# Hybrid decoder trunk, one core: the second merged half turned by VectorE and HBM, the output projection in eight banks and two halves

## The chip, the core and the metric

The program runs on one core of one Trainium2 chip. The core has TensorE (PE in the profile, with PEld for its weight loads), VectorE (DVE), ScalarE (ACT), GpSimd (POOL) and SyncE (SP), which here only issues DMAs. Each engine works through its own list of instructions in order; semaphores make one engine wait for another. PSUM has eight banks of 128 x 512 fp32 values, and TensorE's results land there. The metric is device time in microseconds of one execution, lower is better.

## The reference, cut to what matters

Two layers work on x, 256 tokens by 1024 channels, fp32. A layer is

```python
h = rms_norm(x, attn_norm[l])
p = h @ w_in[l]                                  # split into the branches' inputs and three gates
merged = (sigmoid(g_mla) * (o_mla @ w_branch_mla)
          + sigmoid(g_moba) * (o_moba @ w_branch_moba)
          + sigmoid(g_ret) * (o_ret @ w_branch_ret))
x = x + merged @ w_out[l]                        # the output projection: 256 x 1024 by 1024 x 1024
h = rms_norm(x, mlp_norm[l])
x = x + squared_relu(h @ w_up) @ w_down
```

and a last rms_norm follows. The change touches `merged`, of which the retention branch is the last term, and `merged @ w_out`.

## The kernel before, in words

**Numbers.** fp32 products are made of three passes: each operand is split into a high part (ScalarE, a copy to the type fp32r) and the rest (VectorE, a subtraction), and `three` (L298 to L300) issues high by high, high by low, low by high. A matmul takes a 128 x 128 stationary tile and up to 512 moving columns.

**Weights.** `weight_plan` lays all weights out in HBM in blocks of at most 128 x 1024 fp32 (512 KB), in the order of use. `fetch` brings one block: SP issues the transfer into a `raw` buffer (L210, seven buffers), ScalarE makes `whi` (L277), VectorE makes `wlo` (L279), six buffers each. `load_w` hands a block out and fetches ahead by `AHEAD`; `have(n)` fetches until n blocks are ready or on the way. A raw buffer is free again when its `wlo` is made, a `whi` buffer when TensorE has used the block. `behind[key]` is a list of instructions: when block `key` is fetched, what it issues on the same engine is put behind them (`tc.issue_after`).

**Order.** Instructions are traced in program order; a scheduler then orders each engine's list by a simulated time, those traced earlier first when several are ready. `tc.keep_in_program_order(ins)` puts an instruction behind the one traced before it on its engine. `tc.manual_schedule(engines={PE})` keeps TensorE's order as traced while it is open. `prog` is the list of units of a layer and `at(slot, step)` hangs a step behind a unit.

**The stage in question.** Layer 0 reaches it at about 199 us and layer 1 at about 594 us. Merged is made in two halves of 512 channels. For each half the three branches run (`branch`, six units `bmla0` ... `bret1` of two weight blocks each; t is the half of the tokens, j the weight block, kk one of its two 128-row parts). After the retention branch `merge` adds the branch to the merged half (L715 and L717, on VectorE, once for each t); the result is the tile `th`, tokens on partitions. The projection needs merged with channels on partitions, that is turned.

- The first half is turned by VectorE in 32 x 32 blocks (`turn_row`, L328), written to HBM (`bounce`, L342) and read back in the right places (`mergedturned`, four reads, L348). `merged_split` splits it into `mT[0]` (L319).
- The second half is turned by TensorE: `merged_turn(t)` makes four transposes (L1174) into a PSUM tile `pmt`; ScalarE and VectorE split that into `mT[1]` (L319).
- `wout_first` takes the first four of eight column blocks n (128 columns each, `FIRST`, a weight block `wout n` each): the first half of merged for n = 0 to 3, with `merged_turn(0)` behind n = 1 and `merged_turn(1)` behind n = 2, then the second half for n = 0 to 3, each in its own `acc` bank. `out_part` (L1240) issues, for one n and one half, four matmuls of 512 columns (mT's high and low part side by side, by `whi`) and four of 256 (high by `wlo`); for n = 0 it issues twelve of 256, so that the sum needs no second addition.
- `wout(n)` for n = 4 to 7 takes both halves at once, in banks from `acc` (four banks in all).
- `out_done(n)` adds the bank to x (L1244, VectorE, one instruction for n = 0, two else) and takes the MLP's split input `xs` from it (L314 on ScalarE, L315 on VectorE) and its squares (L382, L385, and L387 and L389 for their sum).
- TensorE's order is as traced from `bret1` to the end of `wout_first`; behind it the scheduler mixes `wout` 4 to 7 with the first MLP blocks (`up`, tile `pup`).

The banks are four of tag `acc` and four of tag `misc`.

Of the kernel before, what the change touches and what calls it, by code (L numbers as in the profile page):

```python
# [7 lines left out]
F32 = mybir.dt.float32  # L8
# [62 lines left out]
def weight_plan():  # L71

    plan = []

    def block(key, name, kt, cols, per):
        for j in range(0, kt, per):
            plan.append(((*key, j // per), name, (j, per), cols))

    def span(c, n):
        return range(c, c + n)  # L80

    for l in range(L):
        if l == 0:

            plan.append(((l, "mq", 0), "w_in", (0, 1), C_MQ))
            plan.append(((l, "b0", 0), "w_in", (0, 1), C_MLA))
            for k in range(1, KD):
                plan.append(((l, "b0mq", k), "w_in", (k, 1), [*C_MLA, *C_MQ]))
        else:
            block((l, "b0"), "w_in", KD, C_MLA, 2)  # L90
            block((l, "mq"), "w_in", KD, C_MQ, 2)
        block((l, "mk"), "w_in", KD, C_MK, 2)
        block((l, "mv"), "w_in", KD, C_MV, 2)
        mv, plan = plan[-4:], plan[:-4]
        for i, (key, name, kt, cols) in enumerate(
            (("qrope", "mla_w_q_up", 2, C_QROPE), ("qnope", "mla_w_q_up", 2, C_QNOPE), ("kvup", "mla_w_kv_up", 1, C_KV))
        ):
            block((l, key), name, kt, cols, kt)
            plan.append(mv[i])
        plan.append(mv[3])  # L100
        for i in range(2):
            block((l, "gmla%d" % i), "w_in", KD, span(C_GMLA + 512 * i, 512), 2)
        for i in range(2):
            block((l, "gmoba%d" % i), "w_in", KD, span(C_GMOBA + 512 * i, 512), 2)
        def branch_block(name, i):
            block((l, "b%s%d" % (name, i)), "w_branch_" + name, 4, span(512 * i, 512), 2)

        block((l, "rqk"), "w_in", KD, C_RQK, 2)
        block((l, "rv"), "w_in", KD, C_RV, 2)
        block((l, "rg"), "w_in", KD, span(C_RG, 512), 2)  # L110
        for i in range(2):
            block((l, "gret%d" % i), "w_in", KD, span(C_GRET + 512 * i, 512), 2)
        for name, i in LATE:
            branch_block(name, i)
        for n in range(KD):
            block((l, "wout", n), "w_out", KD, span(P * n, P), KD)
        for kind, i in mlp_order(l):
            if kind == "up":
                g, j = divmod(i, 4)
                plan.append(((l, "up", g, j), "w_mlp_up", (2 * j, 2), span(512 * g, 512)))  # L120
            else:
                plan.append(((l, "down", i, 0), "w_mlp_down", (i, 1), range(D)))
    at, offset = {}, 0
    for key, name, (j, n), cols in plan:
        at[key] = (offset, n, len(cols))
        offset += P * n * len(cols)
    return plan, at, offset
# [22 lines left out]
def trunk(ctx: ExitStack, tc: tile.TileContext, gx, wts, consts, gfin, gn, xtok, out):  # L150
# [35 lines left out]
    def load_w(*key):  # L186

        ahead = 0 if key[:2] in ((0, "b0"), (0, "mq"), (0, "b0mq")) else AHEAD
        have(min(ahead + 1, len(loaded) + len(order)))
        return loaded.pop(key)  # L190
# [94 lines left out]
    def acc_tile(name="acc"):  # L285
        return ps.tile([P, 512], F32, name=name, tag="acc", bufs=4)

    def misc_tile(name="misc"):
        return ps.tile([P, 512], F32, name=name, tag="misc", bufs=4)
# [28 lines left out]
    def split_plain(src, hi, lo):  # L318
        return nc.scalar.activation(hi, src, AF.Copy), nc.vector.tensor_sub(lo, src, hi.bitcast(F32))  # L319
# [371 lines left out]
    def branch(l, key, parts, oT, th, merged, between=None, then=None):  # L691


        def unit(half, j, accs):
            if j == 0:
                accs.extend(acc_tile() for _ in range(NT))
            if between and half and j == 0:
                between(0)
            wh, wl = load_w(l, f"{key}{half}", j)
            by_k = [(t, kk) for kk in range(2) for t in range(NT)]  # L700
            for t, kk in sorted(by_k) if j else by_k:
                if between and half and j and (t, kk) == (0, 0):
                    between(1)
                if between and half and j and (t, kk) == (1, 0):
                    between(2)
                k, sl = 2 * j + kk, slice(P * t, P * t + P)
                three(accs[t], oT[0][:, k, sl], oT[1][:, k, sl], wh[:, kk, :], wl[:, kk, :], k == 0, k == 3)
                if then and j and kk:
                    then(half, t, [tc.keep_in_program_order(step) for step in merge(half, t, accs[t])])
            for t in range(NT) if j and not then else ():  # L710
                list(merge(half, t, accs[t]))

        def merge(half, t, acc):
            z = th[half, t]
            yield nc.vector.scalar_tensor_tensor(z, z, 1.0, acc, op0=ALU.add, op1=ALU.mult)  # L715
            if (half, t) in merged:
                yield nc.vector.tensor_add(merged[half, t], merged[half, t], z)  # L717
            else:
                merged[half, t] = z

        for half in parts:
            accs = []
            for j in range(2):
                prog.append(((f"{key}{half}", j), lambda half=half, j=j, accs=accs: unit(half, j, accs)))
# [60 lines left out]
    def layer(l, xn, before):  # L785
# [379 lines left out]
        th_ret = gates(l, "gret", xn)  # L1165
        order_out = ExitStack()

        def merged_turn(t):
            if t == 0:

                mT.append(sb.tile([P, 4, 2, S], F32R, name="mT", tag="KK", bufs=1))
            pt = misc_tile("pmt")
            for i in range(4):
                nc.tensor.transpose(pt[:, P * i : P * i + P], merged[1, t][:, P * i : P * i + P], ident)  # L1174
            split_plain(
                pt.rearrange("p (k s) -> p k s", k=4), *(mT[1][:, :, i, P * t : P * t + P] for i in range(2))
            )

        def between(i):

            if i == 0:
                order_out.enter_context(tc.manual_schedule(engines={mybir.EngineType.PE}))

        early = []

        def merged_tile(half, t, steps):


            if half:
                behind.setdefault((l, "wout", 5, 0), []).extend(steps[-1:])  # L1190
                return
            if t == 0:
                early.append(blocks_tile("merged"))
            turned = tc.keep_in_program_order(turn_row(early[0], t, merged[0, t]))
            if t == 1:
                behind[l, "bret1", 0] = [turned]
                early.append(turned_by_hbm(early[0], "merged", "t4", T4, (l, "wout", 5, 0)))

        def merged_split():
            mT.append(sb.tile([P, 4, 2, S], F32R, name="mT", tag="Q", bufs=1))  # L1200
# [25 lines left out]

        xm = []

        def out_part(w, acc, half, wide, n=4):


            ks = [(k, mT[k // 4][:, k % 4]) for k in range(4 * half, 4 * half + n)]
            if wide:
                jobs = [(acc, w[0][:, k, :], m.rearrange("p two s -> p (two s)")) for k, m in ks]
                jobs += [(acc[:, :S], w[1][:, k, :], m[:, 0, :]) for k, m in ks]
            else:
                jobs = [(acc[:, :S], w[i][:, k, :], m[:, 0, :]) for k, m in ks for i in range(2)]
                jobs += [(acc[:, :S], w[0][:, k, :], m[:, 1, :]) for k, m in ks]
            for i, (o, a, b) in enumerate(jobs):
                nc.tensor.matmul(o, a, b, start=half == 0 and i == 0, stop=4 * half + n == KD and i == len(jobs) - 1)  # L1240

        def out_done(n, acc):
            for i in range(2 if n else 1):
# [2 lines left out]
                )  # L1246
            xm[0].take(n)

        def wout(n):
            w, acc = load_w(l, "wout", n, 0), acc_tile()  # L1250
            out_part(w, acc, 0, True, KD)
            out_done(n, acc)

        def wout_first():
            xm.append(Normed(G_MLP + KD * l, KD))
            some = [(load_w(l, "wout", n, 0), acc_tile()) for n in range(FIRST)]
            for half in range(2):
                for n, (w, acc) in enumerate(some):
                    out_part(w, acc, half, n > 0)
                    if half == 0 and n in (1, 2):  # L1260
                        merged_turn(n - 1)
            for n in range(FIRST):
                out_done(n, some[n][1])
            order_out.close()

        prog.append((("wout", 0), wout_first))
        for n in range(FIRST, KD):
            prog.append((("wout", n), lambda n=n: wout(n)))
        run()
        xm = xm[0]  # L1270

# [321 lines left out]
W2K = 17  # L1593
WARM = 8
SMALL = 16
FIRST = 4
AHEAD = 1
GAP = 8

# [90 lines left out]
```

## Time and profile before

| what | us |
|---|---|
| time, median of 3 runs | 802.19 (801.83 to 802.56) |
| the profiled execution's own time | 801.34 |
| its span, first to last instruction | 799.2 |
| TensorE busy | 792.5 |
| VectorE busy | 655.9 |
| ScalarE busy | 493.4 |
| TensorE's transposes of the second half, 16 of them, first and last start | 206.7 and 604.2 |

Times in views are microseconds from the span's start, and durations of one instruction stand beside them. Matmuls overlap: one of 512 columns takes 0.39 us from start to end, and the next starts 0.23 us after it. So the cost of a matmul is read from the distance of starts, or from the chain of work that ended last, which counts each only for the time that it adds. The SP queue's rows show when a transfer is issued; the table of DMA issues has the median time from issue to landing.

### The profile page before, as it was taken

The numbers are of one execution on the slowest core, as the hardware profiler recorded it, in microseconds if no ns is written. First come the engines' busy times: TensorE is split into PE (matmuls) and PEld (weight loads), VectorE is DVE, ScalarE is ACT, GpSimd is POOL, SyncE is SP. The second block draws the span as 40 slices with busy tenths as digits, with TensorE's granted clock in tenths as the row PEclk, the third lists the DMA queues.
The fourth block names the chain that finished last, engine by engine and source line by source line (L and its number), as shares of the span: only waits on it lengthen the run. The fifth ranks groups of instructions, "written<-read, shape, count | busy, mean of one in ns | idle before, by whom it ended". The sixth has DMA issues, their size and how long they took to land.

```text
span 799.2 us, 11136 instructions
## 1 busy us (share of the span) xinstructions
PE 792.5 (99%) x3818; PEld 659.2 (82%) x3818; DVE 655.9 (82%) x1131; ACT 493.4 (62%) x750; POOL 29.0 (4%) x32
## 2 busy tenths in 40 slices
PE   9999999999999999999999999999999999999997
PEld 7888887888888888888888888888888888888885
DVE  6789678878888888887796976788698879899785
ACT  7786665544557666665477865654545666666563
POOL 0100000000030000000020000000000300000000
PEclk9999999999999999999999999999999999999999
DMA  9969968965677876776745989598666687688751
GB/s 333 375 229 298 305 224 233 312 217 174 222 218 236 283 224 229 265 265 223 251 163 197 289 281 301 181 280 252 221 231 183 195 284 262 223 287 297 265 185 53
DMA packets 70280, 194.74 MB, mean 244 GB/s; under 512 B 8016, under 2 KB 27856, under 8 KB 70224
## 3 DMA queue, kind: packets, MB, share of 16 engines
q1 hardware_dynamic: 69648, 193.17, 73.6%
q10 hardware_dynamic: 576, 0.87, 0.3%
q8 instruction: 30, 0.49, 0.3%
q14 instruction: 26, 0.21, 0.1%
HBM read 171.46 MB, written 22.02 MB: 242 GB/s over the span
## 4 chain that ended last, share of the span: by engine, by line
PE 99%; DVE 0%; issue 0%; ACT 0%
PE acc L298 19%; PE acc L300 19%; PE acc L299 19%; PE pup L298 8%; PE pup L300 8%; PE pup L299 8%; PE acc L1240 6%; PE acc L859 1%; PE ps_s L1005 1%; PE po L645 1%; PE ps_s L551 1%; PE warm L765 0%; PE po L647 0%; PE ps_r L551 0%; PE b L866 0%; PE b L865 0%
## 5 line engine op out<-in xcount | busy, mean ns | idle before, releaser
L277 ACT ACTIVATE whi<-raw 128x1024 fp32r<-128x1024 f32 (+3 forms) x263 | 264.8, 1019 | 164.6 <-PE acc L300 101.4
L279 DVE TENSOR_TENSOR wlo<-raw,whi 128x1024 fp32r<-128x1024 f32 (+3 forms) x263 | 305.3, 1176 | 70.2 <-ACT whi L277 66.7
L298 PE MATMUL acc<-whi,xs 128*128 128x512 f32 (+1 forms) x384 | 150.0, 392 | 0.0
L299 PE MATMUL acc<-wlo,xs 128*128 128x512 f32 (+1 forms) x384 | 149.4, 389 | 0.0
L300 PE MATMUL acc<-whi,xs 128*128 128x512 f32 (+1 forms) x384 | 149.0, 389 | 0.0
L299 PE MATMUL pup<-wlo,xs 128*128 128x512 f32 x256 | 99.8, 390 | 0.0
L300 PE MATMUL pup<-whi,xs 128*128 128x512 f32 x256 | 99.6, 389 | 0.0
L298 PE MATMUL pup<-whi,xs 128*128 128x512 f32 x256 | 99.4, 389 | 0.0
L298 PEld LDWEIGHTS acc<-whi,xs 128*128 128x128 f32 x384 | 72.1, 188 | 15.7 <-ACT whi L277 0.7
L300 PEld LDWEIGHTS acc<-whi,xs 128*128 128x128 f32 x384 | 72.1, 188 | 14.3
L299 PEld LDWEIGHTS acc<-wlo,xs 128*128 128x128 f32 x384 | 72.1, 188 | 14.0
L300 PE MATMUL acc<-whi,sq 128*128 128x512 f32 x184 | 71.9, 391 | 0.0
L298 PE MATMUL acc<-whi,sq 128*128 128x512 f32 x184 | 71.8, 390 | 0.0
L299 PE MATMUL acc<-wlo,sq 128*128 128x512 f32 x184 | 71.6, 389 | 0.0
L300 PEld LDWEIGHTS pup<-whi,xs 128*128 128x128 f32 x256 | 48.1, 188 | 9.9
L299 PEld LDWEIGHTS pup<-wlo,xs 128*128 128x128 f32 x256 | 48.1, 188 | 9.9
L298 PEld LDWEIGHTS pup<-whi,xs 128*128 128x128 f32 x256 | 47.9, 188 | 9.7
L300 PEld LDWEIGHTS acc<-whi,sq 128*128 128x128 f32 x184 | 34.5, 188 | 7.8 <-DVE sq L319 0.6
L299 PEld LDWEIGHTS acc<-wlo,sq 128*128 128x128 f32 x184 | 34.5, 188 | 7.2
L573 ACT ACTIVATE prob<-prob,smx 128x128 f32<-128x128 f32 x64 | 28.4, 444 | 19.6 <-DVE smx L570 19.5
L298 PEld LDWEIGHTS acc<-whi,sq 128*128 128x128 f32 x184 | 34.6, 188 | 6.9
L1240 PE MATMUL acc<-mT,whi 128*128 128x512 f32 (+1 forms) x144 | 35.2, 371 | 0.0
(278 smaller groups left out, 1204.0 us busy)
## 6 DMA issues: line engine op xcount, KB each, us to landing
raw<-wts SPq DMA_DIRECT2D x264, 512.0 KB, 5.0
bounce<-hblocks SPq DMA_DIRECT2D x16, 512.0 KB, 3.8
hturned<-bounce SPq DMA_DIRECT2D x64, 128.0 KB, 3.1
pbounce<-blocks SPq DMA_DIRECT2D x8, 768.0 KB, 5.8
probT<-pbounce SPq DMA_DIRECT2D x32, 192.0 KB, 5.5
raw<-wts SPq DMA_DIRECT2D x5, 464.0 KB, 6.1
raw<-wts SPq DMA_DIRECT2D x4, 416.0 KB, 4.7
dec<-consts SPq DMA_DIRECT2D x2, 768.0 KB, 7.7
```

The costliest lines, as they stand in the source:

```text
L277: fetched.append(nc.scalar.activation(hi[:, cs], raw[:, cs], AF.Copy))
L279: nc.vector.tensor_sub(lo[:, cs], raw[:, cs], hi[:, cs].bitcast(F32))
L298: nc.tensor.matmul(o, ah, bh, start=start, stop=False, **more)
L299: nc.tensor.matmul(o, ah, bl, start=False, stop=False, **more)
L300: nc.tensor.matmul(o, al, bh, start=False, stop=stop, **more)
L551: mm = nc.tensor.matmul(bank[:, o], a[rows, sa], b[rows, sb_], start=True, stop=True)
L573: nc.scalar.activation(p[:, a:b], p[:, a:b], AF.Exp, bias=m[:, 2 + i : 3 + i], scale=d**-0.5, accum_out=m[:, 4 + i : 5 + i])
L645: nc.tensor.matmul(dst, vh, pT[h + j][0], start=True, stop=False)
L859: nc.tensor.matmul(mq[t][:, cs], a[:, P * t : P * t + P], wq[part][:, cs], start=first, stop=stop)
L1005: nc.tensor.matmul(bank[:, o], mla["Q"][:, h, qs], mla["K"][:, h, ks], start=True, stop=True)
L1240: nc.tensor.matmul(o, a, b, start=half == 0 and i == 0, stop=4 * half + n == KD and i == len(jobs) - 1)
```

## The change

It has four parts.

1. **Last branch by rows.** `bret1` now keeps both weight blocks (`ws`): with the first block it works on token half t = 0 alone, with the second it finishes t = 0 and then does all of t = 1. The sum of t = 0 is complete twelve matmuls before the end of the branch, where it was six.
2. **Second half turned by VectorE and HBM.** For each t, `merged_tile` turns the merged half in 32 x 32 blocks into `late` (one instruction, behind the additions), and SP writes it to HBM (256 KB). `late_fetch` reads it back, four reads of 64 KB for each t, in pieces of 128 values (512 bytes); all reads stand behind the second write in SP's list. `late_split` splits it into `mT[1]`, ScalarE's part behind the `whi` of weight block (1, 1). The eight transposes on TensorE in each layer, and the PSUM tile `pmt`, are gone.
3. **Output projection in eight banks.** Weight blocks are cut anew: four for the first half of merged and four for the second, each with 256 columns. TensorE does the first half of merged for all eight n, then the second half for all eight, in four `misc` and four `acc` banks, and `out_done(n)` follows each n of the second half.
4. **Order.** The manual order of TensorE's list reaches from `bret1` to the end of the projection; `up` blocks no longer come between. `behind` of block (1, 1), sixth of the eight like `wout 5` before, holds the first half's write and both turns, where it held the first half's write and the additions.

```diff
-        for n in range(KD):
-            block((l, "wout", n), "w_out", KD, span(P * n, P), KD)
+        for half in range(2):
+            for m in range(KD // 2):
+                plan.append(((l, "wout", half, m), "w_out", (4 * half, 4), span(2 * P * m, 2 * P)))
...
-            if between and half and j == 0:
-                between(0)
-            wh, wl = load_w(l, f"{key}{half}", j)
-            by_k = [(t, kk) for kk in range(2) for t in range(NT)]
-            for t, kk in sorted(by_k) if j else by_k:
...
-                k, sl = 2 * j + kk, slice(P * t, P * t + P)
+            if between and j == 0:
+                between()
+            ws[half, j] = load_w(l, f"{key}{half}", j)
+            if not between:
+                jobs = [(t, j, kk) for t in range(NT) for kk in range(2)]
+                jobs = jobs if j else sorted(jobs, key=lambda job: job[2])
+            else:
+                jobs = [(t, i, kk) for t, i in ((1, 0), (1, 1)) for kk in range(2)] if j else []
+                jobs = [(0, j, kk) for kk in range(2)] + jobs
+            for t, i, kk in jobs:
+                k, sl = 2 * i + kk, slice(P * t, P * t + P)
+                wh, wl = ws[half, i]
...
             if half:
-                behind.setdefault((l, "wout", 5, 0), []).extend(steps[-1:])
+                if t == 0:
+                    late.append(blocks_tile("merged"))
+                cs = slice(2 * S * t, 2 * S * t + 2 * S)
+                turn = nc.vector.transpose(late[0][:, cs].rearrange("p (b j e) -> p j b e", b=4, j=4), merged[1, t])
+                tc.keep_in_program_order(turn)
+                late.append(dr.tile([P, 2 * S], F32, name="mbounce", bufs=NT))
+                wrote.append(nc.sync.dma_start(late[-1], late[0][:, cs]))
+                behind.setdefault((l, "wout", 1, 1), []).append(turn)
                 return
...
+        def late_fetch():
+            turned = sb.tile([P, 4 * S], F32, name="mergedturned", tag="t4", bufs=T4)
+            for t in range(NT):
+                cs = slice(2 * S * t, 2 * S * t + 2 * S)
+                for b in range(4):
+                    src = late[1 + t].rearrange("(a p) (b r) -> b p a r", a=4, b=4)[b]
+                    with tc.issue_after(wrote[1].ins):
+                        nc.sync.dma_start(turned[32 * b : 32 * b + 32, cs].rearrange("p (a r) -> p a r", a=4), src)
+            return turned
+
+        def late_split(turned):
+            mT.append(sb.tile([P, 4, 2, S], F32R, name="mT", tag="KK", bufs=1))
+            have(2)
+            with tc.issue_after(fetched[-1].ins):
+                for t in range(NT):
+                    src = turned[:, 2 * S * t : 2 * S * t + 2 * S].rearrange("p (a j e) -> p j a e", a=4, j=4)
+                    split_plain(
+                        src,
+                        *(mT[1][:, :, i, P * t : P * t + P].rearrange("p j (a e) -> p j a e", a=4) for i in range(2)),
+                    )
+
+        def wout():
             xm.append(Normed(G_MLP + KD * l, KD))
-            some = [(load_w(l, "wout", n, 0), acc_tile()) for n in range(FIRST)]
+            turned = late_fetch()
+            accs = [misc_tile("pwo") if n < 4 else acc_tile() for n in range(KD)]
             for half in range(2):
-                for n, (w, acc) in enumerate(some):
-                    out_part(w, acc, half, n > 0)
-                    if half == 0 and n in (1, 2):
-                        merged_turn(n - 1)
-            for n in range(FIRST):
-                out_done(n, some[n][1])
+                for m in range(KD // 2):
+                    w = load_w(l, "wout", half, m)
+                    for i in range(2):
+                        n = 2 * m + i
+                        out_part(w, accs[n], half, n > 0, slice(P * i, P * i + P))
+                        if half:
+                            out_done(n, accs[n])
+                if half == 0:
+                    late_split(turned)
             order_out.close()
```

More of the change, by code (lines that the diff above doesn't have):

```diff
@@ L691, in branch @@
     def branch(l, key, parts, oT, th, merged, between=None, then=None):
+        ws = {}
         def unit(half, j, accs):
@@ L696, in unit @@
                 accs.extend(acc_tile() for _ in range(NT))
-            if between and half and j == 0:
-                between(0)
-            wh, wl = load_w(l, f"{key}{half}", j)
-            by_k = [(t, kk) for kk in range(2) for t in range(NT)]
-            for t, kk in sorted(by_k) if j else by_k:
[L702 to L705, printed above, removed]
-                k, sl = 2 * j + kk, slice(P * t, P * t + P)
+            if between and j == 0:
[10 more added lines that the diff above has]
+                wh, wl = ws[half, i]
                 three(accs[t], oT[0][:, k, sl], oT[1][:, k, sl], wh[:, kk, :], wl[:, kk, :], k == 0, k == 3)
-                if then and j and kk:
+                if then and k == 3:
                     then(half, t, [tc.keep_in_program_order(step) for step in merge(half, t, accs[t])])
@@ L1166, in layer, with between @@
         order_out = ExitStack()
[L1168 to L1184, printed above, removed]
+        def between():
+            order_out.enter_context(tc.manual_schedule(engines={mybir.EngineType.PE}))
+        early, late, wrote = [], [], []
         def merged_tile(half, t, steps):
             if half:
-                behind.setdefault((l, "wout", 5, 0), []).extend(steps[-1:])
+                if t == 0:
[6 more added lines that the diff above has]
+                behind.setdefault((l, "wout", 1, 1), []).append(turn)
                 return
@@ L1196, in merged_tile @@
                 behind[l, "bret1", 0] = [turned]
-                early.append(turned_by_hbm(early[0], "merged", "t4", T4, (l, "wout", 5, 0)))
+                early.append(turned_by_hbm(early[0], "merged", "t4", T4, (l, "wout", 1, 1)))
         def merged_split():
@@ L1227, in layer, with out_part @@
         xm = []
-        def out_part(w, acc, half, wide, n=4):
-            ks = [(k, mT[k // 4][:, k % 4]) for k in range(4 * half, 4 * half + n)]
+        def out_part(w, acc, half, wide, cs):
+            ks = [(k, mT[half][:, k]) for k in range(4)]
             if wide:
-                jobs = [(acc, w[0][:, k, :], m.rearrange("p two s -> p (two s)")) for k, m in ks]
-                jobs += [(acc[:, :S], w[1][:, k, :], m[:, 0, :]) for k, m in ks]
-            else:
-                jobs = [(acc[:, :S], w[i][:, k, :], m[:, 0, :]) for k, m in ks for i in range(2)]
-                jobs += [(acc[:, :S], w[0][:, k, :], m[:, 1, :]) for k, m in ks]
+                jobs = [(acc, w[0][:, k, cs], m.rearrange("p two s -> p (two s)")) for k, m in ks]
+                jobs += [(acc[:, :S], w[1][:, k, cs], m[:, 0, :]) for k, m in ks]
+            else:
+                jobs = [(acc[:, :S], w[i][:, k, cs], m[:, 0, :]) for k, m in ks for i in range(2)]
+                jobs += [(acc[:, :S], w[0][:, k, cs], m[:, 1, :]) for k, m in ks]
             for i, (o, a, b) in enumerate(jobs):
-                nc.tensor.matmul(o, a, b, start=half == 0 and i == 0, stop=4 * half + n == KD and i == len(jobs) - 1)
+                nc.tensor.matmul(o, a, b, start=half == 0 and i == 0, stop=half == 1 and i == len(jobs) - 1)
         def out_done(n, acc):
@@ L1247, in out_done @@
             xm[0].take(n)
[L1249 to L1254, printed above, removed]
+        def late_fetch():
[7 more added lines that the diff above has]
+            return turned
@@ L1262, in wout_first @@
-            for n in range(FIRST):
-                out_done(n, some[n][1])
+                for m in range(KD // 2):
[7 more added lines that the diff above has]
+                    late_split(turned)
             order_out.close()
-        prog.append((("wout", 0), wout_first))
@@ L1267, in layer @@
-        for n in range(FIRST, KD):
-            prog.append((("wout", n), lambda n=n: wout(n)))
+        prog.append((("wout", 0), wout))
         run()
@@ L1595 @@
 SMALL = 16
-FIRST = 4
 AHEAD = 1
```

## The prediction

> **What bounds the kernel now.** I read the page first, then TensorE's waits, then the chain that ended last inside the stage, then the other engines' timelines there.
>
> ```profile
> span 799.2 us, 11136 instructions
> PE 792.5 (99%) x3818; PEld 659.2 (82%) x3818; DVE 655.9 (82%) x1131; ACT 493.4 (62%) x750; POOL 29.0 (4%) x32
> ...
> PE 99%; DVE 0%; issue 0%; ACT 0%
> ```
>
> ```profile
> PE warm L765 <- PEq L1683: 0.8, 1, 0.8
> ```
>
> The chain is TensorE for 99% of the span, and the list of its waits holds this one row, at the start. Of the 6.7 us that TensorE isn't busy (799.2 - 792.5), 0.8 is that wait and most of the rest the end of the program. So nothing can be won but the time of TensorE instructions that are dropped, and any wait put into TensorE's list is lost in full. The stage itself, layer 0, in the chain (start, us, what):
>
> ```profile
> 204.03 2.84 PE acc L1240 x20
> 206.86 0.44 PE pmt L1174 x4
> 207.30 1.40 PE acc L1240 x8
> 208.70 0.44 PE pmt L1174 x4
> 209.14 9.85 PE acc L1240 x60
> ...
> 219.45 5.57 PE acc L1240 x32
> ...
> 225.96 2.77 PE acc L1240 x16
> ```
>
> The reader is to see that each start is the one before plus its time: from the end of the last branch at 204.03 on, projection and transposes follow each other with no gap (the row left out is the first two MLP matmuls). Layer 1 has the same stage 395.4 us later:
>
> ```profile
> 599.43 2.84 PE acc L1240 x20
> ```
>
> Whatever holds for one layer counts twice.
>
> **What is removed.** Two groups of four transposes at 0.44 us: 0.88 us in each layer, 1.76 us in all. That is the whole gain on offer. The work that split `pmt` lay beside matmuls and is replaced by splits of the same shapes.
>
> **What is moved on TensorE.** The projection keeps its columns, but n = 4 to 7 are cut into halves. A half for one n costs 1.40 us (the row of 8 matmuls), so two cost 2.80; both halves at once take 2.77 to 2.79 (16 in 2.77, 32 in 5.57). At 0.01 to 0.03 for each of four n that is up to 0.1 us a layer; against it, `up` matmuls no longer come between projection groups, worth a few hundredths. I take 0.08 lost. The branch's matmuls only change order, and each still accumulates into its bank three at a time and starts 0.23 us behind the one before (203.64 and 203.86 below). Net: 0.80 us a layer gained, 1.6 in all, if nothing waits.
>
> **What is added, and the one wait that matters.** The second half of merged must now be turned, written, read and split before TensorE has done the first half for all eight n. That first half takes 2.84 for n = 0 and 1, and six times 1.40: 11.24 us. TensorE issued the branch's last matmul at 203.64 and the projection's first at 203.86:
>
> ```profile
> 203.64 0.39 PE L300 MATMUL acc<-whi,oretl 128*128 128x512 f32 x1
> 203.86 0.28 PE L1240 MATMUL acc<-mT,whi 128*128 128x256 f32 x1
> 203.98 0.28 PE L1240 MATMUL acc<-mT,wlo 128*128 128x256 f32 x1
> ```
>
> So `mT[1]` is wanted at 215.10: the high part at once, for both t. n = 0 uses the high part in its first eight matmuls, 0.12 us apart, and the low part from 216.06. Now the chain to it, with VectorE's list of before:
>
> ```profile
> 187.83 0.71 DVE L328 STREAM_TRANSPOSE mergedblocks<-th 128x512 f32<-128x512 f32 x1
> 188.47 0.65 DVE L715 SCALAR_TENSOR_TENSOR th<-th,acc 128x512 f32<-128x512 f32 x1
> ```
>
> ```profile
> 201.68 1.28 DVE L319 TENSOR_TENSOR mT<-mergedturned,mT 128x512 fp32r<-128x512 f32 x2
> 202.88 1.22 DVE L279 TENSOR_TENSOR wlo<-raw,whi 128x1024 fp32r<-128x1024 f32 x1
> 204.02 0.68 DVE L715 SCALAR_TENSOR_TENSOR th<-th,acc 128x512 f32<-128x512 f32 x1
> 204.73 0.69 DVE L717 TENSOR_TENSOR th<-th 128x512 f32<-128x512 f32 x1
> 205.34 0.68 DVE L715 SCALAR_TENSOR_TENSOR th<-th,acc 128x512 f32<-128x512 f32 x1
> 206.06 0.69 DVE L717 TENSOR_TENSOR th<-th 128x512 f32<-128x512 f32 x1
> 206.67 1.22 DVE L279 TENSOR_TENSOR wlo<-raw,whi 128x1024 fp32r<-128x1024 f32 x1
> ```
>
> One t costs VectorE, start to start, 0.71 for the gate, 0.61 for the sum (204.02, 204.73, 205.34) and 0.64 for the turn (187.83 to 188.47): 1.96. The bank of t = 0 is now complete twelve matmuls before the end, at 204.03 - 12 x 0.23 = 201.3. Its chain is pinned behind the splits of `mT[0]`, after which VectorE is free at 202.88, and being traced earlier it goes before the `wlo` that stood there. So t = 0 runs 202.88 to 204.84, t = 1 from there to 206.80, its turn ending 0.07 later (0.71 for 0.64). The two weight splits follow; TensorE needs those blocks at 215.1 and 217.9, so their delay is hidden.
>
> Then SP. No row has these transfers; the nearest:
>
> ```profile
> bounce<-mergedblocks SPq DMA_DIRECT2D x2, 512.0 KB, 2.9
> mergedturned<-bounce SPq DMA_DIRECT2D x8, 128.0 KB, 3.1
> ...
> qkoth<-qr SPq DMA_DIRECT2D x8, 64.0 KB, 2.1
> ...
> y<-y SPq DMA_DIRECT2D x2, 256.0 KB, 2.5
> ```
>
> ```profile
> 193.93 1.75 SPq L348 DMA_DIRECT2D mergedturned<-bounce  x4
> ```
>
> The write of 256 KB lies between 2.5 (same size, alone) and 2.9 (512 KB): I take 2.5, issued at 206.9, landed 209.4. The reads of t = 0 are issued while it flies. Those of t = 1 start at 209.4; four issues take 1.75, so the last starts 1.31 after the first, at 210.7. A read lies between 2.1 (64 KB) and 3.1 (128 KB, in the same scattered pattern); I take 3.1, the nearer pattern: landed 213.8. Then the splits:
>
> ```profile
> L319 ACT ACTIVATE mT<-pmt x4: 599/599/600, 207.3 to 604.6; 128x512 fp32r<-128x512 f32 x4
> L319 DVE TENSOR_TENSOR mT<-pmt,mT x4: 692/692/693, 208.0 to 605.2; 128x512 fp32r<-128x512 f32 x4
> ```
>
> High part ready at 213.8 + 0.6 = 214.4, low part at 215.1. Against 215.10 and 216.06 that leaves 0.7 and 1.0 us. With the short ends the spare is 1.7, with the long end of the write 0.3. **No wait, but by less than one VectorE instruction of 1.2 us.**
>
> **What is late next.** During the second half VectorE must run eight `out_done` (rows of the tile x and of `xs`, ns):
>
> ```profile
> L1244 DVE SCALAR_TENSOR_TENSOR GX<-acc,GX x7: 416/417/425, 212.0 to 221.2; 128x256 f32<-128x256 f32 x7
> L315 DVE SCALAR_TENSOR_TENSOR xs<-GX,xs x4: 476/482/977, 214.6 to 224.4; 128x256 fp32r<-128x256 f32 x4
> ```
>
> 15 additions at 0.42 and eight splits at 0.48 are about 10 us, and four `wlo` at 1.14 (202.88 to 204.02) 4.6: some 14 us in 11.2, a little less where neighbours overlap. It falls behind by about 3 us. This is covered: the first `up` block wants only `xs` 0 and 1, and each further pair is wanted 2.7 us later (twelve matmuls at 0.23). Without this cover the price would be those 3 us a layer. The weights have more cover: SP sends a block when a `raw` buffer is free, and the transfers in the stage left room (columns: span, PE, PEld, DVE, ACT, POOL, clock, DMA share, GB/s):
>
> ```profile
> 204.00:216.00 12.00, 12.00 (x81) 10.93 (x80) 8.51 (x15) 6.18 (x9) 0.00 (x0) 1.00 0.47 150
> 216.00:229.00 13.00, 13.00 (x74) 11.35 (x73) 13.00 (x22) 8.71 (x15) 5.12 (x4) 1.00 0.78 239
> ```
>
> The added 512 KB out and 512 KB in each layer fall where DMA is busy 0.47 of the time. SP itself now stands about 3 us for each wait on a write; behind it are weight loads for blocks that TensorE wants 10 us later.
>
> **A page that speaks against it.** The reads were 3.1 us in the same pattern with runs of 1 KB. The Trainium skill, VectorE: DVE Perf Modes, section The three transpose paths, says that a plain DMA which turns by strides is 19 times slower than the chip's transpose path when the innermost destination stride is large. The trace speaks for the kernel: VectorE has turned the blocks, the DMA moves whole runs, 512 bytes here.
>
> **The rivals.**
> *A. The reads stand behind weight loads (slower).* SP's reads of t = 1 wait for the write until 209.4. In that time two weight splits end (206.8 + 1.14 and + 2.28: 208.0 and 209.1), each freeing a `raw` buffer, and SP sends a load at once when one is free, as here right behind the `wlo` of 206.67:
>
> ```profile
> 207.91 0.33 SPq L210 DMA_DIRECT2D raw<-wts  x1
> ```
>
> If the scheduler put loads between write and reads, each moves the reads by its 512 KB, 1.40 us at the rate of the second, fastest slice, 375 GB/s:
>
> ```profile
> GB/s 333 375 229 298 305 224 233 312 217 174 222 218 236 283 224 229 265 265 223 251 163 197 289 281 301 181 280 252 221 231 183 195 284 262 223 287 297 265 185 53
> ```
>
> One load uses up the spare and 0.7 more; two cost 2.1 a layer; three 3.5. From a wait of 0.80 a layer the change loses, from 1.6 by more than 0.2%: two loads give 801.34 - 1.6 + 4.2 = 803.9, three 806.7. For it: the times meet. Against it: the reads are traced before those loads, and elsewhere SP stands idle between write and read rather than slip a load in, 3.2 us on average:
>
> ```profile
> SPq L348 <- DMA bounce<-hblocks: 51.8, 16, 4.5
> ```
>
> A wait has a second price. The matmuls of the start were paced 0.44 us apart for the same 512 columns that later go every 0.23 (3.54 us for eight):
>
> ```profile
> 0.78 3.54 PE warm L765 x8
> ```
>
> The Trainium skill, TensorE: Matmul & The Clock Gate, section What's actually happening, has the clock halved after an idle window of about 3.4 us; by it, a wait that long would cost another 1.7 us, an estimate. Only three loads or more come near it.
>
> *B. Partly given back.* One weight split (1.14 us) gets between the chains of t = 0 and t = 1, or one load before the reads: high part 0.4 to 0.7 late, gain left 0.1 to 0.4 a layer, 800.6 to 801.1 for this execution.
>
> *C. A second half of TensorE work is dearer than counted*, or `xs` comes late after all: the 3 us of VectorE's backlog would then show before `up`. Up to 3 us a layer, 805.7. Against it: 8 us of cover for the last pair.
>
> *D. The reads are slow of themselves.* The slowest scattered read of the table is this one:
>
> ```profile
> probT<-pbounce SPq DMA_DIRECT2D x32, 192.0 KB, 5.5
> ```
>
> At 5.5 us the high part is there at 216.8, 1.7 late: 801.34 - 1.6 + 3.4 = 803.1. Against it: three times the bytes. By the rule of the Trainium skill, VectorE: DVE Perf Modes, The three transpose paths, nineteen times 0.17 us (64 KB at 375 GB/s) for eight reads would be 26 us, an estimate that ends near 840; the 3.1 us of the same pattern leave it no more than 1 in 100.
>
> **How the numbers follow.** Forecast: 801.34 - 1.6 = 799.7 for an execution like the profiled one; that one lay 0.85 under the median of the three runs (802.19), so for the median 800.6. A measurement of this kernel can tell about 0.2%, 1.6 us, from no change: the forecast stands on that line, and half of its chance falls on each side. Forecast, no wait: 0.55 (own range 800.0 to 801.1 for the median), of it 0.30 faster and 0.25 same. B: 0.22, all but 0.02 same. A: 0.14, slower 0.12. C: 0.01 and D: 0.03, slower (D by a hair). Something gained that I don't see, such as a shorter end of the stage: 0.05, faster. Sums: faster 0.37, same 0.47, slower 0.16. The range reaches down to 799.5 and up to A with two loads, 804.8 for the median (803.9 + 0.85).
>
> **What would show it.** The tile `pmt` gone and TensorE's list of waits still one row: the forecast. A row in that list for L1240 behind ScalarE's or VectorE's `mT`, from `mergedturned`, about 10 us after each last branch: A or B; SP's timeline between `mbounce` and `mergedturned` tells which, by a `raw` row there. VectorE's two turns at about 204.2 and 206.2, with or without a `wlo` between, show whether the start of my chain holds. A landing time over 3.1 us for the reads, or over 2.9 for the write, would break it.

## The result, and the profile after

| | before | after |
|---|---|---|
| median | 802.00 us (801.80 to 802.56, 5 runs) | 810.91 us (809.69 to 813.09, 5 runs) |
| ratio, 95% interval | | 1.0114 [1.0104, 1.0125] |
| profiled execution, its span | 801.34, 799.2 us | 809.69, 807.5 us |

The change makes the kernel 1.1% slower, 6 us beyond the upper end of the range. The page of the changed kernel, its first two lines and the chain that ended last:

```profile
span 807.5 us, 11138 instructions
PE 795.6 (99%) x3802; PEld 659.7 (82%) x3802; DVE 659.3 (82%) x1135; ACT 494.3 (61%) x750; POOL 27.2 (3%) x32
...
PE 91%; DMA 3%; DVE 1%; ACT 1%; issue 1%; SPq 1%; POOL 0%; POOLq 0%; ACTq 0%
```

TensorE was 99% of the chain and is now 91%: the end hangs on transfers and on the other engines for some stretches. TensorE has 16 instructions less, the transposes, and yet 3.1 us more of busy time. Its list of waits (total, times, longest) says where:

```profile
PE acc L299 <- ACT sq L320: 4.8, 2, 2.4
...
PE pwo L1238 <- ACT mT L320: 0.2, 1, 0.2
PE acc L301 <- DVE sq L320: 0.2, 1, 0.2
```

The wait that the prediction was about, for `mT`, is the second row shown, and small. The first row isn't in the projection at all. It is the first `down` of the MLP in each layer, 40 us later, which waits for `sq`, the squared hidden values of the first group. The matmuls there (start, us; in brackets the idle time and what ended it), and the same stretch by windows (columns as in the prediction; the number behind POOL's (x0) is the granted clock):

```profile
254.66 0.39 PE L301 MATMUL pup<-whi,xs 128*128 128x512 f32 x1
257.48 0.66 PE L299 MATMUL acc<-whi,sq 128*128 128x512 f32 x1 [2.43 <-ACT sq L320]
...
258.74 0.79 PE L301 MATMUL acc<-whi,sq 128*128 128x512 f32 x1 [0.17 <-DVE sq L320]
259.33 0.63 PE L299 MATMUL acc<-whi,sq 128*128 128x512 f32 x1
259.75 0.63 PE L300 MATMUL acc<-wlo,sq 128*128 128x512 f32 x1
```

```profile
254.00:257.50 3.50, 1.07 (x6) 0.57 (x4) 1.35 (x3) 1.14 (x2) 0.00 (x0) 1.00 1.05 237
257.50:261.00 3.50, 3.33 (x7) 2.17 (x8) 3.15 (x5) 1.16 (x2) 0.00 (x0) 0.52 0.95 360
```

Two matmuls that should start 0.23 us apart start 2.82 apart (257.48 - 254.66): 2.59 lost. Then the clock is at 0.52 for 3.5 us, and matmuls of 512 columns start 0.42 apart (259.33, 259.75): 3.5 x 0.48 = 1.7 lost. With 0.17 for the low part that is 4.45 in a layer, 8.9 in both. The stage before shows 0.32 for `mT` (below), say 0.6 in both layers, and started 0.55 later, at 204.58 in place of 204.03, with the same list ahead of it (the 0.55 is there from 62 us on, long before the stage). 8.9 + 0.6 + 0.55 less the 1.6 that was forecast is about 8.4; the spans differ by 8.3. So the gain is there, and the MLP eats it more than five times over.

How does `sq` come late? The chain of the changed kernel, from the first group's relu on:

```profile
240.15 0.75 ACT relu L1321 x2
...
241.31 1.07 ACT whi L278
242.41 0.55 DVE wlo L280
...
243.55 0.71 DVE hblocks L329
244.25 1.11 DVE wlo L280
245.36 0.63 DVE hblocks L329
246.01 5.82 DMA bounce<-hblocks
...
253.16 3.10 DMA hturned<-bounce
256.37 1.07 ACT sq L320
```

And the same work in the kernel before: ScalarE's, VectorE's and SP's timelines, the tile `sq`, and TensorE's first use of its low part:

```profile
239.53 1.25 ACT L1305 ACTIVATE relu<-pup,ms 128x512 f32<-128x512 f32 x2
240.66 1.15 ACT L1307 ACTIVATE relu<-relu 128x512 f32<-128x512 f32 x2
...
252.56 1.05 ACT L319 ACTIVATE sq<-hturned 128x1024 fp32r<-128x1024 f32 x1
```

```profile
241.86 1.30 DVE L328 STREAM_TRANSPOSE hblocks<-relu 128x512 f32<-128x512 f32 x2
```

```profile
243.18 0.33 SPq L342 DMA_DIRECT2D bounce<-hblocks  x1
246.96 1.75 SPq L348 DMA_DIRECT2D hturned<-bounce  x4
```

```profile
L319 DVE TENSOR_TENSOR sq<-hturned,sq x1: 1182/1182/1182, 253.9 to 253.9; 128x1024 fp32r<-128x1024 f32 x1
```

```profile
255.18 0.50 PE L300 MATMUL acc<-whi,sq 128*128 128x512 f32 x1
```

Before, the relus, the squares and the turns stood back to back on their engines, the write took 3.8 us (243.18 to 246.96), and the low part of `sq` was ready at 253.9 + 1.18 = 255.1 for a matmul at 255.18: **in time by 0.1 us.** That is the margin of this one instruction. The transfers ahead of it had somewhat more: the trace has the slowest read landed at 251.6, and ScalarE, at other work until then, took it up at 252.56. After, a weight split (`whi` on ScalarE, its `wlo` on VectorE) stands ahead of each square and each turn, so the write starts 246.01 - 240.15 = 5.9 us after the relu, not 3.7, and takes 5.8. For the last, SP's list offers a reason, which the first run below tests: the load of up block 13, which stood behind the write before. It is issued when the `wlo` of 244.25 is done, 0.6 us ahead of the write:

```profile
245.39 0.33 SPq L211 DMA_DIRECT2D raw<-wts  x1
```

### The profile page after: what moved, and what is told of

It reads as the page before. It is cut to its first block, busy times and chain, and to the rows that moved or that the text cites. A ratio compares the mean times of both kernels' runs of the same rounds, so it can differ in the third digit from the quotient of the medians.

```text
span 807.5 us, 11138 instructions
## 1 busy us (share of the span) xinstructions
PE 795.6 (99%) x3802; PEld 659.7 (82%) x3802; DVE 659.3 (82%) x1135; ACT 494.3 (61%) x750; POOL 27.2 (3%) x32
## 4 chain that ended last, share of the span: by engine, by line
PE 91%; DMA 3%; DVE 1%; ACT 1%; issue 1%; SPq 1%; POOL 0%; POOLq 0%; ACTq 0%
PE acc L299 19%; PE acc L301 19%; PE acc L300 19%; PE pup L299 6%; PE pup L300 6%; PE pup L301 6%; PE pwo L1238 2%; PE acc L864 1%; DMA bounce<-hblocks 1%; PE acc L1238 1%; PE ps_s L1010 1%; PE po L646 1%; DMA hturned<-bounce 1%; PE ps_s L552 1%; SPq L1254 1%
## 5 line engine op out<-in xcount | busy, mean ns | idle before, releaser
L299 PE MATMUL acc<-whi,sq 128*128 128x512 f32 x184 | 73.3, 398 | 4.8 <-ACT sq L320 4.8
L301 PE MATMUL acc<-whi,sq 128*128 128x512 f32 x184 | 72.9, 396 | 0.3 <-DVE sq L320 0.2
L320 DVE TENSOR_TENSOR sq<-hturned,sq 128x1024 fp32r<-128x1024 f32 x16 | 19.6, 1224 | 21.2 <-ACT sq L320 21.2
```

What stands on the lines that cost most here:

```text
L299: nc.tensor.matmul(o, ah, bh, start=start, stop=False, **more)
L301: nc.tensor.matmul(o, al, bh, start=False, stop=stop, **more)
```

## The experiments

Two theories. **O**: with the new projection, the weight work (loads and splits) of later blocks is ordered ahead of the first group's chain, which has no time to spare. **S**: the late turn through HBM holds up SP and the engines, and what comes after is late for that reason. A rival R came later: the eight banks cost something of their own. In the diffs, a key in `behind` makes the load and split of that weight block come after the instruction it is given, on each engine.

**Only the load, put behind the write.**

```
-                waiting[g] = turned_blocks(rows, "h", "t4", T4, (l, "down", 4, 0), [(l, "down", 2, 0)])
+                waiting[g] = turned_blocks(
+                    rows, "h", "t4", T4, (l, "down", 4, 0), [(l, "down", 2, 0)], (l, "up", 3, 1)
+                )
```

> The changed kernel, but the weight load that SP issues just ahead of the first MLP group's write (block up 13) is put behind that write. Theory O (the change altered the order in which SP, ScalarE and VectorE do weight work around the first MLP group, and the chain relu, square, turn, write, read, split now ends after TensorE wants it): the write goes from 5.8 us to about 3.7, the wait of TensorE at the first down falls from 2.6 us to under 1 in each layer, and with it goes most of the slow matmuls behind it: about 804. Theory S (SP stood still for the late turn from 205.9 to 213.7, weights arrive late from then on, and the MLP suffers from that backlog): this order changes nothing of it, 808 or more.

803.40 us (802.76 to 805.35), 1.0022 [1.0012, 1.0031]. One 512 KB load in another place brings back 7.5 of the 8.9 us that the change lost. The write, issued at the same point of the chain, now lands in 3.4 us (SP's timeline):

```profile
246.50 0.33 SPq L343 DMA_DIRECT2D bounce<-hblocks  x1
246.92 0.38 SPq L211 DMA_DIRECT2D raw<-wts  x1
249.90 1.75 SPq L349 DMA_DIRECT2D hturned<-bounce  x4
```

The late turn is still all there, so S falls. What is left in the list of waits is 1.0 for the low part of `sq` and 0.5 for `mT`.

**Only the splits of the first `down` block, put behind the squares and turns.**

```
+                behind.setdefault((l, "down", 0, 0), []).append(squared)
...
-[(l, "down", 2, 0)]
+[(l, "down", 2, 0), (l, "down", 0, 0)]
```

> The changed kernel, but the split of weight block down 0 is put behind the second square on ScalarE and behind the second turn on VectorE; the load that waits for that split's buffer falls behind the write by itself. Theory O: the chain to the first down is some 4 us earlier, no wait at it, and the eight transposes saved in each layer show: 802.0 - 1.7 + 0.7 for the waits on the late turn, about 801. Theory S: weights are late anyway, and holding one back makes it worse or the same: 806 or more, with waits on whi or wlo in the first up blocks.

803.91 us (802.77 to 806.83), 1.0025 [1.0010, 1.0040]: short of the 801 that O gave. The load falls behind the write by itself here, but ScalarE's timeline shows that the split of up block 9 still stands between relu and squares:

```profile
240.09 1.27 ACT L1321 ACTIVATE relu<-pup,ms 128x512 f32<-128x512 f32 x2 [2.41 <-POOL ms L439]
241.25 1.06 ACT L278 ACTIVATE whi<-raw 128x1024 fp32r<-128x1024 f32 x1
242.19 1.15 ACT L1323 ACTIVATE relu<-relu 128x512 f32<-128x512 f32 x2
```

The slowest read of `hturned` took 4.4 us in that run, and TensorE still waited 1.0 for the high and 1.1 for the low part. One split was not all of it.

**Eight banks, but the second half turned by TensorE as before** (no late turn, no `mbounce`; the splits of `mT[1]` from `pmt`).

> Eight banks, both halves over all columns and the last branch by rows, as in the changed kernel, but the second half is turned by TensorE's transposes as before (behind n = 1 and n = 2 of the first half, in banks of tag acc), so that nothing is written, read back or waited for on SP. If the eight banks and the longer fixed order are the cause (theory O): the wait at the first down stays, 808 to 810. If the late turn's hold on SP is the cause (theory S): no wait, about 802, like before.

814.32 us (813.41 to 814.79), 1.0151 [1.0135, 1.0166]: slower than the change itself, and beyond the 808 to 810 that O gave. The wait for `sq` is 6.2 us in two times, the load stands ahead of the write here too, and the write takes 6.6 us. So the loss comes with the eight banks and not with the turn through HBM: S falls a second time.

**The kernel before, with the last branch by rows and nothing else.**

> The kernel before with the last branch by rows alone. Both theories: 802.0 within 0.5, no wait at the first down. If the row order were what upsets the weights' order: 805 or more.

801.92 us (801.51 to 802.38), 0.9998 [0.9989, 1.0008]. The order by rows costs nothing that can be measured.

**The change, with all three pieces held back**: the split of up block 9, that of the first `down` block, and the load.

```
+                for key in ((l, "down", 0, 0), (l, "up", 2, 1)):
+                    behind.setdefault(key, []).append(squared)
                 waiting[g] = turned_blocks(
-                    rows, "h", "t4", T4, (l, "down", 4, 0), [(l, "down", 2, 0)])
+                    rows, "h", "t4", T4, (l, "down", 4, 0),
+                    [(l, "down", 2, 0), (l, "down", 0, 0), (l, "up", 2, 1)], (l, "up", 3, 1),
                 )
```

> The changed kernel with three pieces of weight work held back behind the first group's squares and turns: the split of up block 9, the split of the first down block, and the load of up block 13. Theory O (the loss is weight work put ahead of the first group's chain on ScalarE, VectorE and the queue, so the first down waits): the first run with only the load held back stood at 803.4 with about 1.0 and 0.65 us left at the first down of the two layers and 0.7 and 0.2 us at mT; with the splits behind too the first 1.65 go, so 801.0 to 801.9, and TensorE's list of waits keeps only the mT row. Rival R (eight banks cost something of their own that no order of the weight work takes away): 803 or more, with a wait left at the first down.

801.17 us (800.71 to 802.27), 0.9990 [0.9982, 0.9999]. No row for `sq` is left; the only wait beside the start is `PE pwo` for `mT`, 0.3. O holds, R falls.

**The same, and the projection's block (1, 0) held back behind the late turns.**

```
-                behind.setdefault((l, "wout", 1, 1), []).append(turn)
+                for key in ((l, "wout", 1, 0), (l, "wout", 1, 1)):
+                    behind.setdefault(key, []).append(turn)
```

> As the one before, and the split of block (1, 0) of the projection is held behind the late turns, so that no wlo stands between the gate and the sum of t = 0. Theory O and the forecast's own step for the late turn: the mT waits of 0.3 to 0.7 us in each layer go as well, so 0.6 to 0.9 below the kernel before it: 800.2 to 801.0, which is the forecast. Rival: what the late turn wants is not set by VectorE but by the transfers; then the mT row stays at 0.3 us or more and the time is that of the kernel before it.

**800.04 us (799.47 to 800.62), 0.9974 [0.9964, 0.9984]: faster than both kernels.** The reason is in VectorE's list. First the changed kernel, then this one:

```profile
203.43 0.68 DVE L720 SCALAR_TENSOR_TENSOR th<-th,acc 128x512 f32<-128x512 f32 x1
204.35 1.23 DVE L280 TENSOR_TENSOR wlo<-raw,whi 128x1024 fp32r<-128x1024 f32 x1 [0.24 <-ACT whi L278]
205.50 0.68 DVE L722 TENSOR_TENSOR th<-th 128x512 f32<-128x512 f32 x1
...
208.26 0.71 DVE L1185 STREAM_TRANSPOSE mergedblocks<-th 128x512 f32<-128x512 f32 x1
```

```profile
203.18 0.68 DVE L720 SCALAR_TENSOR_TENSOR th<-th,acc 128x512 f32<-128x512 f32 x1
203.89 0.69 DVE L722 TENSOR_TENSOR th<-th 128x512 f32<-128x512 f32 x1
...
206.66 0.71 DVE L1185 STREAM_TRANSPOSE mergedblocks<-th 128x512 f32<-128x512 f32 x1
```

In the changed kernel a `wlo` slipped between the gate and the sum of t = 0, and with the 0.24 us that it waited for its `whi` the second turn came 4.83 us after the first gate (208.26 - 203.43) instead of 3.48. TensorE's matmuls on both sides show the price:

```profile
215.20 0.63 PE L1238 MATMUL acc<-mT,wlo 128*128 128x256 f32 x4
216.00 0.38 PE L1238 MATMUL pwo<-mT,whi 128*128 128x256 f32 x1 [0.17 <-ACT mT L320]
```

Four matmuls from 215.20, 0.12 apart, put the next at 215.68; it came at 216.00, 0.32 late. In the last version there is no such row. TensorE's list is the same in both, instruction for instruction, so only what it waits for has changed. The page of the last version reads:

```profile
PE 790.9 (99%) x3802; PEld 657.6 (82%) x3802; DVE 658.2 (83%) x1135; ACT 493.3 (62%) x750; POOL 27.2 (3%) x32
...
PE 99%; DMA 0%; ACT 0%; DVE 0%; issue 0%
```

**Four banks and six banks.** The weight blocks keep their new shape, TensorE turns the second half, the branch goes by rows; only the number of columns whose halves are apart differs. The diff of the two runs, the line of each marked:

```
+WOUT = ((0, 0), (0, 1), (1, 0), (1, 1), (0, 2), (1, 2), (0, 3), (1, 3))   # four
+WOUT = ((0, 0), (0, 1), (0, 2), (1, 0), (1, 1), (1, 2), (0, 3), (1, 3))   # six
-            for half in range(2):
-                for m in range(KD // 2):
+            for half, m in WOUT:
```

> Weight blocks of the projection in the new shape and the last branch by rows, but four banks at a time as in the kernel before (columns 0 to 3 in two halves, then 4 to 7 whole) and the second half turned by TensorE. Theory O puts the loss on the eight banks, through the additions to x that start later: here they start as before, so 801.6 to 802.6, no wait at the first down over 0.3 us. Rival (the shape of the blocks or the rows order of the branch makes the lists worse): above 806, as the eight banks with the same blocks did at 814.

803.05 us (802.03 to 804.67), 1.0013 [1.0004, 1.0022]. No wait for `sq`, so the shape of the blocks is not the cause. Half a microsecond above what was expected is explained by another row, `PE pmt` waiting for `th`, 0.8 us in three times: the transposes come early, and a `wlo` stands between gate and sum here as well.

> As the one before, but six banks: columns 0 to 5 in two halves, then 6 and 7. The first addition to x comes 2.8 us later than with four banks and 2.8 earlier than with eight. Theory O: the first group's chain is late by a part of what eight banks make it, 802 to 805, with a wait at the first down between 0 and 2 us. If the loss were a threshold in the queue's order alone (the load ahead of the write), it would be 802, since here that load stays behind the write.

801.98 us (801.62 to 803.06), 1.0001 [0.9992, 1.0010], and no wait but the start's. This goes against the half of O that let the loss grow with the delay. The additions to x start later with each pair of banks (tile GX in the projection of layer 0: before, from 212.0, as a row of the prediction has it; then six banks and the change):

```profile
L1235 DVE SCALAR_TENSOR_TENSOR GX<-pwo,GX x7: 413/418/425, 215.4 to 222.0; 128x256 f32<-128x256 f32 x7
```

```profile
L1242 DVE SCALAR_TENSOR_TENSOR GX<-pwo,GX x7: 418/422/426, 218.1 to 224.7; 128x256 f32<-128x256 f32 x7
```

With six banks they are 3.4 us later than before and nothing is lost; relu and squares stand back to back and the load is behind the write. With eight, the order tips. Over these three the loss is a step and not a slope.

**The kernel before, with its write doubled.** The first group's blocks are first written to a spare place in HBM, then to the one that is read. No engine's list changes but SP's.

```
+            if twice:
+                spare = dr.tile([P, 4 * S], F32, name="spare", bufs=1)
+                pinned.enter_context(tc.issue_after(nc.sync.dma_start(spare, blocks).ins))
             wrote = nc.sync.dma_start(bounce, blocks)
```

> The kernel before with one thing added: the first group's blocks are written to HBM twice, first to a spare place that nobody reads, so that 512 KB stand on the queue right ahead of the write that counts. The lists of TensorE, VectorE and ScalarE stay as they were. Theory O (the first down takes the end of the first group's chain, and the chain has no cover to spare in the kernel before): the write that counts takes 5.8 to 6.6 us in place of 3.7, so the first down waits 2 to 3.5 us in each layer and the matmuls behind it are paced slower, 3 to 6 us a layer: 808 to 814. Rival (the stage has cover of its own, and what the changed kernel loses comes from its lists): under 803.5.

804.85 us (804.75 to 805.02), 1.0035 [1.0022, 1.0049]. SP's timeline and TensorE's waits:

```profile
243.78 0.33 SPq L345 DMA_DIRECT2D spare<-hblocks  x1
244.16 0.42 SPq L346 DMA_DIRECT2D bounce<-hblocks  x1
...
248.84 1.74 SPq L352 DMA_DIRECT2D hturned<-bounce  x4
```

```profile
PE acc L300 <- DVE sq L319: 1.1, 2, 0.5
...
PE acc L298 <- ACT sq L319: 0.5, 1, 0.5
```

The kernel before loses 2.8 us from this alone. The time lies between the two forecasts: above the rival's 803.5, and far under O's 808. The write that counts took 4.7 us (244.16 to 248.84), not 5.8 to 6.6, so the waits are 0.5 each and the clock stays up. An equal write ahead delays less than the loads of the changed kernel do. Nor is the cover none, as O had it: a weight load also slipped between write and reads (247.23), the trace has the slowest read landed at 254.4 in place of 251.6, and TensorE, which ran 0.3 later here before the stage, lost only 1.4 us at the first `down` of layer 0. So 2.6 us of delay cost 1.4, and the transfers of the kernel before had some 1.2 us of cover there.

**The kernel before, with the three pieces held back.**

> The kernel before with the three pieces of weight work held back behind the first group's squares and turns, as in the version of the change that did so. If that version's gain came from the held-back work alone, this would gain too, 800 to 801. Theory O: the kernel before waits nowhere, so there is nothing to win: 801.6 to 802.4, no row for the first down in TensorE's list of waits.

801.68 us (801.55 to 802.20), 0.9997 [0.9988, 1.0006]. Where nothing waits, the order wins nothing; the 2.0 us of the best version are the change's own.

**Eight banks turned by TensorE, with the three pieces held back.**

> Eight banks with the second half turned by TensorE, which lost 12 us, now with the same three pieces of weight work held back. Theory O: the wait at the first down goes and the time is that of the kernel before, 801.6 to 802.6; set beside the version with the late turn and both chains first at 800.0, the difference of 1.6 to 2.4 is what the transposes cost (1.76 by the profile). Rival (eight banks have a price of their own): 804 or more.

802.28 us (801.87 to 802.49), 1.0004 [0.9995, 1.0012], against 814.32 without. With the weight work held back, the eight banks cost nothing that can be measured, and the 2.2 us down to 800.04 are the price of the transposes and what lies around them.

## Why the prediction was wrong

**Right: what can be won, and that a wait is lost in full.** 0.80 us a layer, 1.6 in all: TensorE's busy time goes from 792.5 to 790.9 in the version without waits, and that version's median is 800.04 where the forecast said 800.6. Every wait that was measured went into the time.

**Right, once no weight split stands in its way: the late turn meets its time by less than one VectorE instruction.** In the changed kernel itself it was late by 0.3. In the version without waits, VectorE's chain runs from 203.18 to its second turn at 206.66, the transfers follow, and `mT[1]` shows in the tile's rows and in TensorE's:

```profile
L320 ACT ACTIVATE mT<-mergedturned x2: 632/633/634, 211.9 to 213.9; 128x512 fp32r<-128x512 f32 x2
```

```profile
215.41 0.28 PE L1239 MATMUL pwo<-mT,whi 128*128 128x256 f32 x1
```

213.9 + 0.6 = 214.5 against 215.4: 0.9 to spare, 0.7 forecast. That the two are so near is partly luck. The reads took 1.9 to 2.1 us, nearer to the row of the same size (64 KB, 2.1) than to that of the same pattern (3.1) which I took; the queue's own issues, eight in 3.65 us, take a good part of that back.

**Half right: rival B.** A weight split did get into the chain of the late turn, though between gate and sum of t = 0 and not between the two t, and it cost 0.3 a layer at `mT`. The step of the chain that failed is "being traced earlier it goes before the `wlo` that stood there": only block (1, 1) was held behind the turns, and the `wlo` of block (1, 0) got in. Holding that back too took the median from 801.17 to 800.04; side by side, TensorE's lists in those two profiled executions part by 0.5 us at `mT` in layer 0 and by 0.3 in layer 1. Rival A didn't happen: no load came between write and reads.

**Wrong: "What is late next".** The step that failed is the sentence on VectorE's backlog, "This is covered: the first `up` block wants only `xs` 0 and 1", and with it "The weights have more cover". It asked only when `up` needs `xs` and when a weight block is needed. It didn't follow what else moves when the work around the projection moves: the order of the weight work on ScalarE, VectorE and SP against the first group's chain, statistic, relu, squares, turns, write, reads, splits, up to the first `down`. The last instruction of that chain was in time by 0.1 us, in the rows of the kernel before that stand above, and its transfers had some 1.2 us of cover; TensorE's empty list of waits hid both. That TensorE waits for nothing was read as room, and there was little. The write alone came 2.2 us later behind the relu and took 2.0 us more. Moving the load back restores 7.5 us, holding back the two splits as well another 2.2.

**Rival C had the sign and the wrong place.** It put the backlog's 3 us ahead of `up`, at 1 in 100 and 805.7. TensorE never waited there.

**The clock's price was sized right, and the idle time that brings it wrong.** I held that only an idle stretch of some 3.4 us comes near. Here 2.4 us of waiting (2.6 between starts) brought 3.5 us at 0.52. The Trainium skill, TensorE: Matmul & The Clock Gate, section What's actually happening, has the window free-running and about 3.4 us long; the length of the slow stretch agrees with that. Its rule that a whole idle window is needed is not what this run shows.

**Open.** Why eight banks tip the order and six don't was not tried further. The orders part at the first relu: ScalarE makes the split of up block 9 ahead of it with six banks (238.91, the relu at 239.87), as in the kernel before (238.56, 239.53), and behind it in the change (the relu at 240.15, the split at 241.31). What tips this is not shown. Only argued is this: the changed kernel's runs spread over 3.4 us, where the kernel before keeps within 0.8 and the best version within 1.2, because what a transfer takes now goes straight into the time.

## What to carry to other kernels

An empty list of waits doesn't say how near the next wait is. Before moving a stage, follow every chain that starts in it through to the instruction that consumes it, and note by how much each is in time; where it is as little as here, say so in the forecast and put the chain ahead of weight work in the order. When a change shortens the bound engine and the time grows, look for the first late consumer far downstream, and move single loads and splits back before giving up the change: here three of them and one more turned 810.9 into 800.0.

## What the hardware showed that was not expected

A short idle stretch costs more than itself, and not always at once: 2.6 us between starts cost 4.45 in all. In the changed kernel the slow clock came right with the first matmul after the wait. With eight banks turned by TensorE it came later (windows, granted clock as above):

```profile
255.00:258.40 3.40, 0.19 (x2) 0.00 (x1) 0.47 (x2) 1.11 (x2) 0.00 (x0) 1.00 1.00 240
258.40:260.30 1.90, 1.38 (x5) 0.85 (x6) 1.90 (x3) 0.90 (x1) 0.00 (x0) 1.00 0.99 315
260.30:263.70 3.40, 3.40 (x10) 2.63 (x9) 1.96 (x4) 0.63 (x1) 0.00 (x0) 0.51 0.99 406
```

An idle of 3.2 us, then 1.9 us at full clock, then 3.4 us at 0.51: the matmuls were already running when the clock fell. In both traces the records of the granted clock have each slow stretch 3.413 us long, and the second, in layer 1, begins 399.36 us after the first, 117 times as much: the clock changed on a fixed grid. That would explain why it fell at once in one kernel and later in the other; how much idle time within a step is enough is not shown. Waits of 0.5 us, as with the doubled write, left the clock at 1.00.

The same write of 512 KB landed in 2.6 us where the last load had been issued 4.3 us earlier (all three pieces held back: 239.31, the write at 243.59), in 3.4 with a load right behind it, in 3.8 in the kernel before, where a load stood 1.2 us ahead, in 4.7 behind an equal write, and in 5.8 and 6.6 us right behind a weight load. The place of one load, ahead of the write or behind it, was worth 2.4 us here, as much as two VectorE instructions of 1.2.
